# Weight splits issued at a unit's last product, with the loads two units ahead

## The chip, the cores and the metric

The kernel runs on one core of one Trainium2 chip. The time is that of one execution in device microseconds, the median of several executions. The engines named here are TensorE (PE; its weight loads are listed apart as PEld), VectorE (DVE), ScalarE (ACT), GpSimd (POOL) and SyncE (SP), which in this kernel issues the DMAs.

## What is computed

One layer of a bidirectional hybrid encoder in float32, on 2048 tokens of 1024 channels. Cut to what matters:

```
h = rmsnorm(x, g_mix)
z = h @ w_in                      # 1024 -> 5648: qk, v, o, gates of the mLSTM, qkv of NA, q of mem, branch gates
h_m   = mlstm forward + mlstm backward, normalised, times sigmoid(o)
h_na  = neighbourhood attention on the 32 x 64 grid, 8 heads
h_mem = cross attention into 256 memory tokens (k, v from mem @ w_mem_kv)
y = g0 * (h_m @ w_proj_mlstm) + g1 * (h_na @ w_proj_na) + g2 * (h_mem @ w_proj_mem)
x = x + y @ w_out
x + square(relu(rmsnorm(x, g_ffn) @ w_up)) @ w_down
```

## The kernel before

**Products in three parts.** Every large product is made at nearly full float32 precision from three faster ones. Each operand is split into a high part (rounded to float32r) and a low part (the rest), and `mm3` (L226) issues high by high (L231), high by low (L232) and low by high (L233). A weight must therefore be split before it can be used.

**Weight units.** The weights of the first two stages lie in HBM as units of 512 KB (128 partitions by 1024 floats; the four `navm` units have 1056). `fetch` (L155) brings one: it takes a raw buffer (tag `wraw`, 3 of them, L164) and a split buffer (tag `wsp`, 5 of them, L165), issues the load on SP (L171), makes the high part on ACT (L175) and the low part on DVE (L176). The load of a unit has to wait until the split three units earlier has read its raw buffer. The split has to wait until the last product with the unit five earlier has been made, since it takes that unit's place.

**Two kinds of units.** For `naqk`, `navm`, `v` and `o`, a set of four units covers 1024 input channels by 512 (528) output channels, and `tok_group` (L471) runs through all four for each of four groups of 128 tokens. So all four units are in use until the last token group; in it, the first unit has its last product after two of the eight steps over k, the second after four, and so on. For `qk` and the branch gates, one unit covers 128 output channels, and `ch_group` (L481) uses it in 8 steps of three matmuls over 512 tokens and is then done with it.

**Stages.** Stage 1 (`phase_1`) runs four blocks of 512 tokens; `block_a` (L490) takes `naqk`, `qk` (4 units), `navm`, `v`, in blocks 2 and 3 the 24 gate units, and `o`. Between the steps of these products `tick` (L106) slips in small pieces of other work: neighbourhood attention (scores, exponentials L1035, transposes copied out at L1052 and L1054, values L1063), memory attention (exponentials L1179) and the norms of q and k. Stage 2 (`phase_2`) makes the gates of blocks 1 and 0 while the mLSTM runs in the ticks. Stage 3 (the projections and the MLP) fetches its units in its own way.

**Order of the work.** PE runs in program order. The order on ACT, DVE, POOL and SP is fixed before the launch by a planner that goes through a time of its own: among the instructions that could start at that time, it gives an engine the one with the lowest number (`cur_priority`, which counts in program order). `fetch` adds `self.later` = 60 to the number of the two split instructions, so that they rank as if they stood 60 instructions further down. Once fixed, every engine works through its list in order: an instruction that must wait holds up those behind it.

**When units are fetched.** `take` (L218) fetches ahead: when it returns n units, it has fetched until 5 more (`AHEAD`) are there. So the five units behind the set that is about to be used stand in the program ahead of that set's first product, loads and splits together, long before the places are free that their splits go into.

**Evictions around the change.** Each group of products ends in PSUM (two banks for `mm` in stage 1) and is copied out by ACT: L503 (`naqk`), L653 (`qk`, into `cz` for the convolution), L518 and L527 (`navm`), L538 (`v`), L555 (`o`), L598 (gates). PE can begin the group after next only once that copy is made.

Of the kernel before, what the change touches and what calls it, by code (L numbers as in the profile page):

```python
# [12 lines left out]
F32 = mybir.dt.float32  # L13
# [21 lines left out]
ORDER_0 = (2, 3, 0, 1)  # L35
WSP, WRAW, AHEAD = 5, 3, 5
NB = S // TB
SCRATCH = 1024
# [41 lines left out]
class Body:  # L80
    def __init__(self, tc, a):
        self.tc, self.nc, self.a = tc, tc.nc, a
        self.n = 0
        self.later, self.ahead = LATER, AHEAD
# [3 lines left out]
        self.wplan, self.wready = self.plan(), []  # L88

# [65 lines left out]
    def fetch(self):  # L155

        nc = self.nc
        entry = self.wplan.pop(0)
        if len(entry) == 3:
            self.wready.append(self.fetch_sums(*entry[:2]))  # L160
            return
        i, nk = entry
        self.n += 1
        raw = self.p_w.tile([128, 1056], F32, name=f"wr_{self.n}", tag="wraw", bufs=WRAW)  # L164
# [3 lines left out]
        raw = raw[:, :n]  # L168

        w = w[:, :2 * n].rearrange("p (k l c) -> p l k c", k=nk, l=2)  # L170
        nc.sync.dma_start(raw, self.a["w_units"][i] if i < first else self.a["w_navm"][i - first])  # L171
# [3 lines left out]
        nc.scalar.activation(w[:, 0], raw, AF.Copy)  # L175
        nc.vector.tensor_tensor(w[:, 1], raw, w[:, 0].bitcast(F32), ALU.subtract)  # L176
        self.tc.cur_priority -= self.later
        self.wready.append(w)

    def fetch_sums(self, i0, i1):  # L180
# [37 lines left out]
    def take(self, n=4):  # L218

        size = lambda: sum(4 if isinstance(w, dict) else 1 for w in self.wready)  # L220
        while (len(self.wready) < n or size() < n + self.ahead) and self.wplan:
            self.fetch()
        w, self.wready = self.wready[:n], self.wready[n:]
        return w

    def mm3(self, out, lhs, rhs, first, last, more=False):  # L226
# [243 lines left out]

    def tok_group(self, lhsT, w, t, cols=slice(0, 512), every=2):  # L471

        p = self.ps("mm")[:, :cols.stop - cols.start]
        for k in range(8):
            wk = w[k // 2]
            self.mm3(p, self.lhs_tok(lhsT, k, t), (wk[:, 0, k % 2, cols], wk[:, 1, k % 2, cols]), k == 0, k == 7)
            if k % every == every - 1:
                self.tick()
        return p

    def ch_group(self, w, rhs, ks=range(8)):  # L481

        p = self.ps("mm")
        for k in ks:
            self.mm3(p, (w[:, 0, k], w[:, 1, k]), (rhs[:, 0, k], rhs[:, 1, k]), k == ks[0], k == ks[-1])
            if k % 2:
                self.tick()
        return p

    def block_a(self, b):  # L490


        nc, a = self.nc, self.a
        hT = self.hT
        w = self.take(4)
        for i, t in enumerate(ORDER_0 if b == 0 else range(4)):
            if i == 0 or b == 0 and i < 3:
                self.trans_x()
            if b == 0 and i == MEM_R:
                self.mem_rms()  # L500
            p = self.tok_group(hT, w, t)
# [13 lines left out]
        for t in range(4):  # L515
# [8 lines left out]
            p = self.tok_group(hT, w, t, slice(256, 528), 4)  # L524
            z = self.t("zm", [128, 256], 4)
# [7 lines left out]
        for t in range(4):  # L533
            if t == PREP_V and b + 1 < NB and b not in GATES_1:
                self.prep_x()
            p = self.tok_group(hT, w, t)
            s = self.ev()
# [10 lines left out]
        for t in range(4):  # L548
            if t:
                self.trans_x()  # L550
            if t < 3:
                self.prep_x()
            p = self.tok_group(hT, w, t)
            s = self.ev()
# [518 lines left out]
    def mem_setup(self):  # L1073
# [7 lines left out]
        for k in range(0, 8, 2):  # L1081
# [129 lines left out]
    def phase_3(self):  # L1211
# [352 lines left out]
```

## Time and profile before

| | |
|---|---|
| median of 3 runs | 3011.54 us (3009.11 to 3012.48) |
| the profiled execution, own time | 3010.98 us |
| its span, first to last instruction | 3009.2 us |
| mean granted TensorE clock | 0.991 |
| DVE busy over the span | 2070.9 us (69%) |
| ACT busy over the span | 1197.8 us (40%) |
| POOL busy over the span | 240.6 us (8%) |

The busy shares are over the whole span. A row of the windows view gives, for one stretch, each engine's busy time with the number of instructions, the granted TensorE clock (1.00 is full speed), the share of time that the DMA engines worked and the rate. In the timeline view a row is start, duration, engine, line, operation, the tiles written and read, the shapes and a count; the bracket at the end gives the idle time of the engine just before, and what ended it. Stage 1 lasts until about 993 us, and the last gate product of the second stage's units is made at about 1413 us.

### The profile page before, as it was taken

What the parts mean: (1) busy time and instruction counts of PE and PEld (TensorE: products, weight loads), DVE (VectorE), ACT (ScalarE), POOL (GpSimd) and SP (SyncE); (2) the same over time, 40 slices, a digit from 0 to 9 for tenths busy, and PEclk for the clock granted to TensorE, in tenths of its full rate; (3) what the DMA queues carried; (4) which work ended last, traced back from release to release, by engine and by line L of the source; (5) the groups of instructions that cost most, each with busy time, mean ns of one, the idle gap of its engine ahead of it and who ended that gap; (6) DMA issues with size and microseconds to landing.
All of it is one profiled execution on the core that took longest, in us unless ns stands there. A gap on an engine that the chain in (4) does not pass through costs nothing.

```text
span 3009.2 us, 41920 instructions
## 1 busy us (share of the span) xinstructions
PE 2923.3 (97%) x15028; PEld 2382.5 (79%) x15028; DVE 2070.9 (69%) x3557; ACT 1197.8 (40%) x2198; POOL 240.6 (8%) x389
## 2 busy tenths in 40 slices
PE   8989999999989889999999999999999999999999
PEld 6878788878877767778888888888778888888887
DVE  6666676457655675764869888765676888885666
ACT  6454544345543343333234333543322433344331
POOL 3020200011000332330000000000000000000000
PEclk9999999999999999999999999999999999999999
DMA  7776668777789766789634444866774444467554
GB/s 269 229 244 198 217 215 256 244 221 213 229 266 287 231 196 211 251 276 320 199 112 165 153 149 151 282 193 226 252 236 138 137 154 154 154 215 230 191 186 165
DMA packets 341713, 632.97 MB, mean 210 GB/s; under 512 B 29345, under 2 KB 151009, under 8 KB 341505
## 3 DMA queue, kind: packets, MB, share of 16 engines
q1 hardware_dynamic: 341504, 630.30, 65.2%
q8 instruction: 118, 1.93, 0.3%
q14 instruction: 91, 0.74, 0.1%
HBM read 453.63 MB, written 176.55 MB: 209 GB/s over the span
## 4 chain that ended last, share of the span: by engine, by line
PE 58%; DVE 2%; DMA 1%; issue 0%; ACT 0%; SPq 0%; POOL 0%; DVEq 0%; ACTq 0%; POOLq 0%
PE mm L231 19%; PE mm L233 18%; PE mm L232 18%; PE pn L861 1%; PE pn L864 1%; PE mm L1327 0%; DMA wr<-in_w_units_dram 0%; PE mx L870 0%; DVE ev L1483 0%; DVE h L899 0%; DMA hf<-s_hf 0%; DVE acc L1476 0%; DMA X<-s_a 0%; DMA og<-s_o 0%; DVE ws L176 0%
## 5 line engine op out<-in xcount | busy, mean ns | idle before, releaser
L231 PE MATMUL mm<-X,ws 128*128 128x512 f32 x1152 | 448.5, 389 | 0.0
L233 PE MATMUL mm<-X,ws 128*128 128x512 f32 x1152 | 448.2, 389 | 0.0
L232 PE MATMUL mm<-X,ws 128*128 128x512 f32 x1152 | 448.1, 389 | 0.0
L231 PE MATMUL mm<-hT,ws 128*128 128x512 f32 x896 | 378.2, 422 | 12.2 <-ACT cz L653 5.5
L233 PE MATMUL mm<-hT,ws 128*128 128x512 f32 x896 | 355.7, 397 | 0.0
L232 PE MATMUL mm<-hT,ws 128*128 128x512 f32 x896 | 354.8, 396 | 0.6 <-DMA hT<-s_hT 0.6
L232 PE MATMUL mm<-X 128*128 128x512 f32 x896 | 348.8, 389 | 4.4 <-DVE X L1450 4.4
L233 PE MATMUL mm<-X 128*128 128x512 f32 x896 | 348.7, 389 | 0.5 <-DVE X L1450 0.5
L231 PE MATMUL mm<-X 128*128 128x512 f32 x896 | 348.6, 389 | 0.0
L176 DVE TENSOR_TENSOR ws<-wr,ws 128x1024 fp32r<-128x1024 f32 (+1 forms) x212 | 260.8, 1236 | 120.1 <-ACT ws L175 119.0
L1449 ACT ACTIVATE X<-X 128x1024 fp32r<-128x1024 f32 x176 | 187.0, 1062 | 322.9 <-DMA X<-s_t 133.4
L1450 DVE TENSOR_TENSOR X<-X 128x1024 fp32r<-128x1024 f32 x176 | 214.4, 1223 | 133.6 <-ACT X L1449 129.1
L175 ACT ACTIVATE ws<-wr 128x1024 fp32r<-128x1024 f32 (+1 forms) x212 | 223.3, 1059 | 157.4 <-PE mm L233 92.3
L231 PE MATMUL mm<-ws,hT 128*128 128x512 f32 (+2 forms) x704 | 262.2, 372 | 4.3 <-ACT cz L653 2.4
L233 PE MATMUL mm<-ws,hT 128*128 128x512 f32 (+2 forms) x704 | 250.9, 356 | 2.1 <-DVE hT L433 2.1
L232 PEld LDWEIGHTS mm<-X,ws 128*128 128x128 f32 x1152 | 216.3, 188 | 44.9
L233 PEld LDWEIGHTS mm<-X,ws 128*128 128x128 f32 x1152 | 216.2, 188 | 44.9
L231 PEld LDWEIGHTS mm<-X,ws 128*128 128x128 f32 x1152 | 216.2, 188 | 44.7
L232 PE MATMUL mm<-ws,hT 128*128 128x512 f32 (+2 forms) x704 | 250.3, 355 | 0.3 <-DVE ws L176 0.3
L201 ACT ACTIVATE ws<-wr 128x512 fp32r<-128x512 f32 x224 | 135.0, 628 | 220.3 <-PE mm L233 139.7
L231 PEld LDWEIGHTS mm<-hT,ws 128*128 128x128 f32 x896 | 171.2, 191 | 56.9 <-issue 11.1
L233 PEld LDWEIGHTS mm<-hT,ws 128*128 128x128 f32 x896 | 170.4, 190 | 39.5
(266 smaller groups left out, 4865.2 us busy)
## 6 DMA issues: line engine op xcount, KB each, us to landing
wr<-in_w_units_dram SPq DMA_DIRECT2D x308, 512.0 KB
s_s<-u SPq DMA_DIRECT2D x32, 1024.0 KB
X<-s_s SPq DMA_DIRECT2D x64, 512.0 KB
X<-s_t SPq DMA_DIRECT2D x64, 512.0 KB
s_g<-ev SPq DMA_DIRECT2D x96, 256.0 KB
ev<-s_g SPq DMA_DIRECT2D x96, 256.0 KB
s_a<-u SPq DMA_DIRECT2D x96, 256.0 KB
X<-s_a SPq DMA_DIRECT2D x48, 512.0 KB
```

What stands on the lines that cost most here:

```text
L175: nc.scalar.activation(w[:, 0], raw, AF.Copy)
L176: nc.vector.tensor_tensor(w[:, 1], raw, w[:, 0].bitcast(F32), ALU.subtract)
L201: nc.scalar.activation(hi, src, AF.Copy)
L231: mm(out, lhs[0], rhs[0], start=first, stop=False)
L232: mm(out, lhs[0], rhs[1], start=False, stop=False)
L233: mm(out, lhs[1], rhs[0], start=False, stop=last)
L861: nc.tensor.matmul(pn[h % 2][:, j], pt[:, h], v1[:, h], start=True, stop=first)
L864: nc.tensor.matmul(pn[h % 2][:, j], qw[hp, j], C[hp, j], start=False, stop=True)
L1449: nc.scalar.activation(hi, src, AF.Copy)
L1450: nc.vector.tensor_tensor(lo, src, hi.bitcast(F32), ALU.subtract)
```

## The change

Loading and splitting become two steps. `load` takes a raw buffer and issues the DMA; `fetch` first calls `load` until up to `self.pre` units beyond the one in hand are loaded, and then splits that one. In the first two stages `self.pre` is 2. There `take` fetches only what it returns and lacks, and a new `done` fetches one unit at each place where a unit has had its last product: after every second step of the last token group of a set of four (then with `later` = 0), and at the end of every `ch_group` (with `later` = 60). The instructions, buffers and their numbers stay the same. For the third stage the old way is set again (`pre` = 0, `ahead` = 5). During the memory setup at the start, `take` keeps one unit ahead (`ahead` = 1) in place of five.

```diff
+PRE = 2
-        entry = self.wplan.pop(0)
-        if len(entry) == 3:
+        while len(self.wloaded) <= self.pre and self.wplan and (not self.wloaded or len(self.wplan[0]) == 2):
+            self.load()
+        entry, raw = self.wloaded.pop(0)
+        if raw is None:
             self.wready.append(self.fetch_sums(*entry[:2]))
             return
...
-        nc.sync.dma_start(raw, self.a["w_units"][i] if i < first else self.a["w_navm"][i - first])
...
+    def load(self):
+        entry, raw = self.wplan.pop(0), None
+        if len(entry) == 2:
+            i = entry[0]
+            self.n += 1
+            first = self.a["w_units"].shape[0]
+            raw = self.p_w.tile([128, 1056], F32, name=f"wr_{self.n}", tag="wraw", bufs=WRAW)[:, :1024 if i < first else 1056]
+            self.nc.sync.dma_start(raw, self.a["w_units"][i] if i < first else self.a["w_navm"][i - first])
+        self.wloaded.append((entry, raw))
...
     def take(self, n=4):
+        if self.pre:
+            while len(self.wready) < n:
+                self.fetch()
+            w, self.wready = self.wready[:n], self.wready[n:]
+            return w
...
+    def done(self, urgent=False):
+
+        if self.pre and (self.wplan or self.wloaded):
+            self.later = 0 if urgent else LATER
+            self.fetch()
...
     def tok_group(self, lhsT, w, t, cols=slice(0, 512), every=2, last=False):
...
             if k % every == every - 1:
                 self.tick()
+            if last and k % 2:
+                self.done(True)
...
     def ch_group(self, w, rhs, ks=range(8)):
...
             if k % 2:
                 self.tick()
+        self.done()
         return p
...
     def mem_setup(self):
...
-        self.later = later
+        self.ahead = WSP - 4
         w = self.take(4)
...
+        self.later, self.pre = later, PRE
...
             self.tick()
+            if k % 2:
+                self.done(True)
...
     def phase_3(self):
...
+        self.pre, self.later, self.ahead = 0, LATER, AHEAD
         self.late_gates(lambda: True)
```

`tok_group` is called with `last` set for the last token group of `naqk`, of `v`, of `o` and of the second half of `navm`.

More of the change, by code (lines that the diff above doesn't have):

```diff
@@ L83, in __init__ @@
         self.n = 0
-        self.later, self.ahead = LATER, AHEAD
+        self.later, self.ahead, self.pre = LATER, AHEAD, 0
         self.streams, self.qkq, self.memq, self.aux_end = [], [], [], False
@@ L87, in __init__ @@
         self.jobs = []
-        self.wplan, self.wready = self.plan(), []
+        self.wplan, self.wloaded, self.wready = self.plan(), [], []
     def t(self, tag, shape, bufs, dt=F32):
@@ L163, in fetch @@
         self.n += 1
-        raw = self.p_w.tile([128, 1056], F32, name=f"wr_{self.n}", tag="wraw", bufs=WRAW)
         w = self.p_ws.tile([128, 2112], F32R, name=f"ws_{self.n}", tag="wsp", bufs=WSP)
@@ L167, in fetch @@
         n = 1024 if i < first else 1056
-        raw = raw[:, :n]
         w = w[:, :2 * n].rearrange("p (k l c) -> p l k c", k=nk, l=2)
-        nc.sync.dma_start(raw, self.a["w_units"][i] if i < first else self.a["w_navm"][i - first])
         raw = raw.rearrange("p (k c) -> p k c", k=nk)
@@ L218, in take @@
     def take(self, n=4):
+        if self.pre:
[3 more added lines that the diff above has]
+            return w
         size = lambda: sum(4 if isinstance(w, dict) else 1 for w in self.wready)
-        while (len(self.wready) < n or size() < n + self.ahead) and self.wplan:
+        while (len(self.wready) < n or size() < n + self.ahead) and (self.wplan or self.wloaded):
             self.fetch()
@@ L469, in lhs_tok, with tok_group @@
         return hT[:, 0, k, sl], hT[:, 1, k, sl]
-    def tok_group(self, lhsT, w, t, cols=slice(0, 512), every=2):
+    def tok_group(self, lhsT, w, t, cols=slice(0, 512), every=2, last=False):
         p = self.ps("mm")[:, :cols.stop - cols.start]
@@ L500, in block_a @@
                 self.mem_rms()
-            p = self.tok_group(hT, w, t)
+            p = self.tok_group(hT, w, t, last=i == 3)
             z = self.t("zna", [128, 512], 3)
@@ L523, in block_a @@
                     self.store(self.scr["vna"][half, 8 * b + 2 * t + r], s[p0:p0 + 40])
-            p = self.tok_group(hT, w, t, slice(256, 528), 4)
+            p = self.tok_group(hT, w, t, slice(256, 528), 4, t == 3)
             z = self.t("zm", [128, 256], 4)
@@ L535, in block_a @@
                 self.prep_x()
-            p = self.tok_group(hT, w, t)
+            p = self.tok_group(hT, w, t, last=t == 3)
             s = self.ev()
@@ L552, in block_a @@
                 self.prep_x()
-            p = self.tok_group(hT, w, t)
+            p = self.tok_group(hT, w, t, last=t == 3)
             s = self.ev()
```

## The prediction

> **What bounds the kernel now.** I read the page first, then the windows view by stage, then who PE waited for, and only then single places in the timeline.
>
> ```profile
> span 3009.2 us, 41920 instructions
> PE 2923.3 (97%) x15028; PEld 2382.5 (79%) x15028; DVE 2070.9 (69%) x3557; ACT 1197.8 (40%) x2198; POOL 240.6 (8%) x389
> ```
> ```profile
> 0.00:993.00 993.00, 938.23 (x5802) 767.63 (x5802) 618.33 (x1390) 487.76 (x1016) 110.84 (x217) 0.98 0.77 239
> 993.00:1413.00 420.00, 400.03 (x2183) 304.85 (x2184) 266.03 (x526) 158.33 (x417) 129.72 (x172) 0.98 0.75 241
> 1413.00:3009.00 1596.00, 1585.05 (x7045) 1309.98 (x7043) 1186.55 (x1641) 551.74 (x766) 0.00 (x0) 1.00 0.56 185
> ```
>
> PE bounds it. The part that the change touches, up to 1413 us, has 993 - 938.23 + 420 - 400.03 = 74.7 us of idle PE, and a clock of 0.98 where stage 3 has 1.00. Rows are the stretch, then PE, PEld, DVE, ACT and POOL, then clock, DMA share, GB/s. The whole fund is this: 74.7 us, and about 2% of 1413 us (28 us at most) through the clock. What ended those idle times, up to 1500 us:
>
> ```profile
> PE mx L1063 <- DVE npt L1054: 19.4, 13, 4.6
> PE mm L231 <- ACT cz L653: 7.9, 4, 2.5
> ...
> PE mx L231 <- ACT ws L175: 6.9, 1, 6.9
> PE mx L1030 <- DMA nab<-in_rpb_dram: 5.9, 2, 5.6
> ...
> PE mx L232 <- DVE ws L176: 1.0, 2, 0.6
> ...
> PE mm L232 <- DVE ws L176: 0.3, 1, 0.3
> ```
>
> PE hardly ever waits for a split: apart from the start (6.9 us, 1.0 us) it is 0.3 us. It waits for copies on DVE and ACT, and the splits matter as what stands ahead of these copies in their lists. The group view says how much they hold ACT and DVE (last part: idle before them, and what ended it):
>
> ```profile
> L176 DVE TENSOR_TENSOR ws<-wr,ws 128x1024 fp32r<-128x1024 f32 x167 | 205.5, 1237 | 103.2 <-ACT ws L175 102.2
> L175 ACT ACTIVATE ws<-wr 128x1024 fp32r<-128x1024 f32 x167 | 175.3, 1056 | 95.0 <-DMA wr<-in_w_units_dram 54.6 <-PE mm L233 39.8
> ```
>
> A split costs ACT 1.06 us and DVE 1.24 us, and before 1413 us ACT stood 54.6 us at the head of its list for a load and 39.8 us for PE with a split.
>
> **The change, part by part.** No instruction is added or taken away; three are moved per unit. The number of a split falls back by about one channel group: before, unit u+5 is fetched ahead of the products of u, now behind them. So a copy of the same group, which has its number right behind the group, now goes ahead of the split. The load goes the other way: u+7 is loaded at the end of u, so u+5 at the end of u-2, one unit earlier than at the start of u. On SP it passes the stores and bias loads of a unit. On POOL nothing is passed.
>
> *Split behind the eviction (`qk`, blocks 1 and 2).*
>
> ```profile
> 212.02 1.08 ACT L175 ACTIVATE ws<-wr 128x1056 fp32r<-128x1056 f32 x1
> ...
> 214.44 0.60 ACT L653 ACTIVATE cz<-mm 128x512 f32<-128x512 f32 x1
> ```
> ```profile
> 215.09 0.50 PE L231 MATMUL mm<-hT,ws 128*128 128x512 f32 x1 [2.49 <-ACT cz L653]
> ```
> ```profile
> 365.63 1.08 ACT L175 ACTIVATE ws<-wr 128x1056 fp32r<-128x1056 f32 x1
> ...
> 368.15 0.60 ACT L653 ACTIVATE cz<-mm 128x512 f32<-128x512 f32 x1
> ```
> ```profile
> 368.81 0.50 PE L231 MATMUL mm<-hT,ws 128*128 128x512 f32 x1 [1.62 <-ACT cz L653]
> ```
>
> Here the split waits for the same products as the copy and goes first. Moved behind, it gives back 1.08 us at each place: 2.49 becomes 1.41, 1.62 becomes 0.54. The split itself is for `navm`, two groups later, so nobody waits for it.
>
> What a gap costs beyond itself shows in the granted clock behind it (four stretches of the windows view; the clock is the third number from the end):
>
> ```profile
> 216.25:219.65 3.40, 3.40 (x14) 2.80 (x13) 3.40 (x11) 2.08 (x4) 0.14 (x1) 0.50 0.72 259
> 369.00:372.40 3.40, 3.40 (x20) 2.81 (x19) 3.40 (x10) 1.93 (x6) 0.13 (x1) 1.00 0.55 159
> 875.02:878.43 3.41, 3.41 (x11) 2.48 (x9) 2.60 (x6) 1.03 (x3) 0.00 (x0) 0.50 0.54 153
> 1324.00:1327.40 3.40, 3.40 (x24) 2.65 (x22) 3.40 (x10) 1.72 (x9) 2.47 (x3) 1.00 0.91 267
> ```
>
> After the gap of 2.49 us PE ran 3.40 us at half speed; after 1.62 us it did not. Half of 3.40 is 1.70 us lost. With 1.41 us left this goes: 1.08 + 1.70 + 1.08 = 3.9 us.
>
> [...]
>
> *Split behind the attention copies (372 us).*
>
> ```profile
> 373.98 1.25 DVE L176 TENSOR_TENSOR ws<-wr,ws 128x1056 fp32r<-128x1056 f32 x1
> ...
> 376.89 0.68 DVE L1054 COPY npt<-tr 120x512 f32<-120x512 f32 x1
> ```
> ```profile
> 377.62 1.08 PE L1063 MATMUL mx<-npt,nav 120*32 120x128 f32 x16 [4.56 <-DVE npt L1054]
> ```
>
> DVE does the split ahead of the copy on which PE waits 4.56 us. Behind it: 1.25 us less. The gap stays long, so I count no clock.
>
> *Load one unit earlier (gates).*
>
> ```profile
> 865.47 0.43 SPq L171 DMA_DIRECT2D wr<-in_w_units_dram  x1
> ```
> ```profile
> 871.13 1.06 ACT L175 ACTIVATE ws<-wr 128x1024 fp32r<-128x1024 f32 x1 [3.29 <-DMA wr<-in_w_units_dram]
> ...
> 872.57 0.65 ACT L1035 ACTIVATE nsb<-nsb,sm 128x440 f32<-128x440 f32 x1
> ```
> ```profile
> 874.16 1.14 PE L1063 MATMUL mx<-npt,nav 120*32 120x128 f32 x26 [1.87 <-DVE npt L1054]
> ```
> ```profile
> 912.69 1.06 ACT L175 ACTIVATE ws<-wr 128x1024 fp32r<-128x1024 f32 x1 [1.56 <-DMA wr<-in_w_units_dram]
> ```
> ```profile
> 915.59 0.65 PE L1063 MATMUL mx<-npt,nav 120*32 120x128 f32 x16 [1.54 <-DVE npt L1054]
> ```
> ```profile
> 1321.89 1.06 ACT L175 ACTIVATE ws<-wr 128x1024 fp32r<-128x1024 f32 x1 [6.26 <-DMA wr<-in_w_units_dram]
> ```
> ```profile
> 1323.49 0.66 PE L903 MATMUL tr<-ident,h 128*128 128x128 f32 x4 [1.78 <-ACT de L810]
> ```
>
> The load issued at 865.47 us reached ACT at 871.13, 5.7 us later; meanwhile ACT held up the exponential that the copy and then PE needed. A unit is 24 matmuls. The stretch from 369.00 us, at full clock, holds 20 in 3.40 us, 0.17 us each, short ones among them; so a unit lasts at least 24 x 0.17 = 4.1 us, more than the 3.29 us waited. The wait goes, with the gap and the half-speed window at 875.02: 1.87 + 1.70 = 3.6 us. The other two places, 1.54 and 1.78 us, lie between nothing (an attention copy still waits for its own chain) and all of it, 3.3 us; having no nearer row I take half, 1.7 us.
>
> *Splits at the change from one set to the next.* These had the best possible place, at the head of the list. Now what is ready and has a lower number goes ahead.
>
> ```profile
> 106.83 2.95 ACT L175 ACTIVATE ws<-wr 128x1024 fp32r<-128x1024 f32 x3
> 109.68 0.48 ACT L1179 ACTIVATE me<-mx,sm 128x256 f32<-128x256 f32 x1
> ...
> 110.48 0.22 ACT L1179 ACTIVATION_READ_ACCUMULATOR me<-mx,sm 128x1 f32 x1
> ```
> ```profile
> 109.25 0.50 PE L232 MATMUL mm<-ws,hT 128*128 128x512 f32 x1 [0.32 <-DVE ws L176]
> ```
>
> From `navm` to `v` in block 0 there is no slack: PE waits 0.32 us for the first of three splits made back to back. Two exponentials stand just behind them, 110.48 + 0.22 - 109.68 = 1.02 us. If these come first, PE waits 1.0 us more. There are four such changes, one per block. Lower bound nothing, upper bound two pairs at all four, 4 x 2.04 = 8.2 us. I take one pair at the one place without slack, 1.0 us.
>
> *SP.* The loads now reach SP as soon as a raw buffer is free by the planner's time, and SP stands until it is free in fact. This happens already:
>
> ```profile
> SPq L171 <- DVE ws L176: 113.5, 58, 7.3
> ```
>
> One such wait is 113.5 / 58 = 2.0 us, and the stores and bias loads (L1014) stand behind it; PE already waits 5.9 us for such a bias. Most of it is covered by the double-buffered evictions; without this cover, all of a wait reaches PE. I take one, 2.0 us; the bounds are nothing and three, 6 us.
>
> *The rest costs nothing:* `take` and the memory setup issue the same instructions; raw buffers limit the first loads as before. Stage 3 is set back to the old way.
>
> **The sum:** gains 3.9 + 1.25 + 3.6 + 1.7 = 10.4 us; costs 1.0 + 2.0 = 3.0 us; net -7.4 us. Against the profiled execution's own 3010.98 us that gives 3003.6; it lies 0.56 us below the median of the runs, so 3004.1, said as 3004 us.
>
> **The rivals.**
>
> *A: nothing moves.* The engines' lists come from readiness in the planner's time, and a number decides only between instructions that are ready together. With ACT at 40% there is seldom a choice. For it: the 39.8 us that ACT waits for PE show that splits start as soon as their place is free. Against: 212.02 and 365.63, where a choice existed. Small gains and losses cancel: 3011 us, give or take 6.
>
> *B: the splits come too late; slower.* At the change of sets, two exponential pairs get ahead in all four blocks: 8.2 us, with one half-speed window (the gap then passes 1.87 us) 1.7 us, and none of the gains: 3011.5 + 9.9 = 3021 us. It decides once more than the slack stands ahead of the split, and in block 0 that slack is nothing. For it: 109.25, and DVE with 205.5 us of splits in 1413. Against: the sets are split with `later` = 0.
>
> *C: SP stands.* The early loads hold up bias loads and gate stores: three waits, 6 us, half the gains (5.2 us) and the 1.0 us above: 3011.5 + 1.8 = 3013 us.
>
> *D: no clock comes back.* The half-speed windows have another cause than these gaps, so that shortening 2.49 and 1.87 us leaves them: 3004.1 + 3.4 = 3007.5 us. Against it: both windows at 0.50 begin within 1.2 us of the end of such a gap. [...]
>
> **How the numbers follow.** About 0.2%, 6 us, is what a measurement can tell from no change. The forecast has 0.45 (0.40 below 3005.5, 0.05 within), A 0.25 (0.06, 0.15 and 0.04 faster, within, slower), B 0.17 (slower), C 0.08 (half within, half slower), D 0.05 (within). Faster 0.46, within 0.29, slower 0.25. Low end: all gains with the halved ones whole (12.1), a second window at 377 us (1.7) and no cost, 2997.7, and as much again as the two `cz` gaps that I left out (7.9 - 2.49 - 1.62 = 3.8 us) with a window: 2992. High end: B, 3021. Outside lie some 0.07 below and 0.12 above. The forecast's own range is 2997 to 3007.
>
> **What would show it.** Right: ACT's wait for loads in L175 falls well below 54.6 us; `cz` stands ahead of the split in `qk`; fewer windows at 0.50; PE's waits for L653 and L1054 fall below 27.3 us together. Wrong: new PE waits for L175 or L176 at the first group of `v` or `naqk` (B), for `nab` or L598 (C), or a wait list as before (A).

## The result, and the profile after

| | before | after |
|---|---|---|
| median | 3010.99 us (4 runs, 3009.11 to 3012.48) | 3031.65 us (4 runs, 3030.57 to 3037.03) |
| ratio, 95% interval | | 1.0071 (1.0058 to 1.0084) |
| the profiled execution, own time | 3010.98 us | 3037.03 us |
| its span | 3009.2 us | 3035.3 us |

The change costs 20.7 us by the medians. The forecast was 3004, its range 2992 to 3021. One of the ten executions of g1_gates, an experiment described below, took 7413.52 us; its ratio leaves that execution out, its median does not. The profiled execution of after is the longest of its four, 5.4 us above their median, so losses read from its trace add up to somewhat more than 20.7.

In after's lines L252, L253 and L254 are the three matmuls of `mm3` (L231 to L233 before), L187 is the load, L1078 the copy `npt` on DVE, L1062 the scaled scores `nsb` (L1038 before), L677 `cz`, L622 the gates' eviction. First the windows by stage, of after; the columns are those explained above.

```profile
0.00:993.00 993.00, 935.90 (x5793) 765.04 (x5794) 617.64 (x1388) 484.33 (x1013) 109.24 (x217) 0.98 0.77 237
993.00:1413.00 420.00, 386.82 (x2088) 293.73 (x2087) 272.78 (x526) 156.23 (x413) 132.63 (x172) 0.95 0.72 224
1413.00:3009.00 1596.00, 1591.49 (x7063) 1315.41 (x7062) 1178.24 (x1626) 557.34 (x773) 0.00 (x0) 1.00 0.57 188
```

PE's idle time in the same stretches of time is 57.1 us in place of 54.8, and 33.2 us in place of 20.0, where the clock fell from 0.98 to 0.95. Stage 3 comes later and is otherwise the same. Which engine ended PE's waits up to 1500 us, of after (total, times, longest):

```profile
PE mx L1087 <- DVE npt L1078: 23.3, 14, 4.2
...
PE mm L252 <- DMA hT<-s_hT: 8.8, 3, 7.8
...
PE mm L252 <- ACT cz L677: 5.0, 2, 3.5
PE mx L795 <- DVE C L900: 4.8, 2, 2.8
PE mx L894 <- DVE hm L930: 4.6, 4, 2.6
...
PE mx L850 <- DVE C L900: 4.2, 3, 1.5
PE mm L253 <- DVE ws L176: 3.2, 4, 1.6
```

Three kinds are new or grown: the wait for a DMA of `hT` (8.8 us), those of the mLSTM for `C` and `hm` (4.8 + 4.6 + 4.2 us; 2.7 us before, shown with g6_rank2 below), and those for splits L176 in the main products (3.2 us, 0.3 before). The waits for `cz` and `npt`, which the change was to shorten, are 28.3 us together against 27.3.

What the change does to ACT came out as foreseen. The groups view of 0 to 1413 us, after and then before; behind the last bar is the idle time just before these instructions and what ended it:

```profile
L175 ACT ACTIVATE ws<-wr 128x1024 fp32r<-128x1024 f32 (+1 forms) x180 | 189.6, 1059 | 18.6 <-PE mm L254 8.5 <-DMA wr<-in_w_units_dram 8.2 <-DMA wr<-in_w_navm_dram 1.5
```
```profile
L175 ACT ACTIVATE ws<-wr 128x1024 fp32r<-128x1024 f32 (+1 forms) x183 | 192.6, 1058 | 98.2 <-DMA wr<-in_w_units_dram 54.6 <-PE mm L233 41.6 <-DMA wr<-in_w_navm_dram 1.4
```

ACT's idle time ahead of splits fell from 98.2 to 18.6 us, that for loads from 54.6 to 8.2. That idle time was not what bound the kernel.

**Where the time goes.** Both traces have the same 15028 matmul records in the same order. The start of the n-th of them in one profile, less its start in before's, is the lag of that profile at this point of the work. Worked out so, in us (the points are before's times; the other kernels are described below):

```
point           100   400   450   600   650   700   950  1000  1100  1200  1350  1400
after           6.3   3.4   7.9  12.0  15.9  11.8   5.3   9.9   9.5  12.2  24.4  23.7
e7_memold       1.4  -2.1  -1.5  -2.3   6.5   1.9  -5.2  -0.2  -1.3  -1.6   7.3   6.7
k1_close        0.2  -1.9  -1.3  -1.6   5.0   1.9  -4.5  -8.9  -3.1  -3.1  -0.8  -1.4
g1_gates        1.7  -0.4  -0.4  -1.2   0.2  -2.0  -7.1  -5.9  -6.1  -5.2  -3.8  -3.6
g4_behind      -1.7   1.2   1.5   0.4   0.4   0.3  -1.1  -1.8  -1.5  -1.5   0.6   1.5
g6_rank2       -0.9   1.3   1.4   0.7   1.8   1.0   0.2  -0.2  -0.1   2.4   5.7   8.3
p1_later70     -1.8   3.2   4.7   3.6   3.6   5.9   0.0  -0.1   2.0   2.9   5.8   5.9
p3_later65      0.8  -0.9   3.4   2.3   2.3   0.9  -4.1  -4.3  -4.8  -3.9  -2.7  -3.2
```

Read the row of after: a loss at the start, two between 400 and 600 us, one at 650; then, between 650 and 950 us, 10.6 us come back (most of it where the gates run); then 4.6 us at 1000 us and 12.2 between 1200 and 1350. A lag is that of one execution: from 674 us on, the operations, by their tiles, stand in the same order on ACT, DVE, POOL and SP in after and e7_memold, and yet from 700 to 1400 us the one loses 11.9 us and the other 4.8. So a few us between two rows are no price of a part. Four places, with their lines.

*The start.* ACT, then PE, of after, and ACT of before (timeline view):

```profile
20.27 1.05 ACT L359 ACTIVATE xq<-xstage 128x1024 bf16<-128x1024 f32 x1
...
24.51 1.04 ACT L175 ACTIVATE ws<-wr 128x1024 fp32r<-128x1024 f32 x1
```
```profile
25.60 0.50 PE L252 MATMUL mm<-ws,hT 128*128 128x512 f32 x1 [0.84 <-ACT ws L175]
26.86 0.50 PE L253 MATMUL mm<-ws,hT 128*128 128x512 f32 x1 [0.76 <-DVE ws L176]
```
```profile
19.80 1.05 ACT L175 ACTIVATE ws<-wr 128x1024 fp32r<-128x1024 f32 x1
```

Since `take` now keeps one unit ahead in the memory setup in place of five, three units of the first `naqk` are fetched in the product loop, behind the calls of `prep_x` in the program. So their splits rank behind the norm preparation of the first tokens (L359, L362), which is ready and takes ACT from 20.27 to 24.51. The first products wait for these splits. By 100 us the lag is 6.3 us, one gap of 3.46 us at `cz` with two half-speed windows behind it included (before has 2.36 us there and one window).

*From `o` to `naqk` (block 3).* PE of after:

```profile
662.23 0.50 PE L252 MATMUL mm<-ws,hT 128*128 128x512 f32 x1 [0.37 <-ACT ws L175]
664.36 0.50 PE L253 MATMUL mm<-ws,hT 128*128 128x512 f32 x1 [1.63 <-DVE ws L176]
```

The last split of the set comes too late, 2.0 us. But before had two waits for `nsb` just there, 2.00 us at 653.48 and 2.55 us at 659.68 us, which after does not have: the lag falls again by 700 us.

*The reload of `hT`.* SP's queue and PE of after, then SP and PE of before:

```profile
993.53 3.05 SPq L187 DMA_DIRECT2D wr<-in_w_units_dram  x3
...
997.15 5.89 SPq L589 DMA_DIRECT2D hT<-s_hT  x8
```
```profile
1003.00 0.77 PE L252 MATMUL mm<-hT,ws 128*128 128x512 f32 x1 [7.78 <-DMA hT<-s_hT]
```
```profile
988.16 0.34 SPq L171 DMA_DIRECT2D wr<-in_w_units_dram  x1
988.60 0.45 SPq L565 DMA_DIRECT2D hT<-s_hT  x1
...
990.99 3.51 SPq L565 DMA_DIRECT2D hT<-s_hT  x7
```
```profile
993.17 0.47 PE L231 MATMUL mm<-hT,ws 128*128 128x512 f32 x1 [3.32 <-issue]
994.21 0.58 PE L232 MATMUL mm<-hT,ws 128*128 128x512 f32 x1 [0.56 <-DMA hT<-s_hT]
```

At the end of stage 1 the input of the next gates is brought back in eight pieces, and PE waits for it. In after three loads of weights stand ahead of them on SP, each waiting for the split that frees its raw buffer (3.3 us for the three), and the first of the eight pieces leaves 3.6 us after the first load does. Before there was one load; the first piece left 0.4 us after it and the other seven 2.8 us after it, behind a store. PE waits 7.78 us in place of 3.88 (3.32 + 0.56; what ended the 3.32 us the profile doesn't tell).

*The mLSTM in stage 2.* DVE and PE of after, then DVE of before at the same point of the work:

```profile
1263.36 0.68 DVE L930 TENSOR_TENSOR hm<-tr,hm 128x512 fp32r<-128x512 f32 x1
1264.53 0.69 DVE L916 TENSOR_TENSOR h<-h,hf 128x512 f32<-128x512 f32 x1 [0.48 <-DMA hf<-s_hf]
...
1268.00 1.47 DVE L923 SCALAR_TENSOR_TENSOR h<-h,rs,og 128x128 f32<-128x128 f32 x1 [1.11 <-POOL rs L345]
...
1271.36 0.59 DVE L900 SCALAR_TENSOR_TENSOR C<-C,wb,mx 128x129 f32<-128x129 f32 x2
```
```profile
1272.10 0.38 PE L795 MATMUL mx<-ident,r_m 4*128 4x4 f32 x4 [1.96 <-DVE C L900]
```
```profile
1247.03 0.68 DVE L892 TENSOR_TENSOR h<-h,hf 128x512 f32<-128x512 f32 x1
...
1248.77 0.68 DVE L906 TENSOR_TENSOR hm<-tr,hm 128x512 fp32r<-128x512 f32 x1
```

The next chunk of the mLSTM waits for the state update `C`. On DVE, `C` stands behind `h` (L923), which waits for POOL's `rs`; `rs` is made from ACT's squares of the sum `h` (L916). Before, DVE made that sum ahead of `hm` and of the split, in after behind `hm`: 17.5 us later in its trace than in before's, where PE is 14.7 us later. So the chain ends later for PE, which waits 1.96 us here where it had no wait before. By the three rows of the wait list above such waits are 13.6 us, against 2.7 before.

### The profile page after: what moved, and what is told of

Same layout as the page of the kernel before. It is cut to its first block, busy times and chain, and to the rows that moved or that the text cites. A ratio compares the mean times of both kernels' runs of the same rounds, so it can differ in the third digit from the quotient of the medians.

```text
span 3035.3 us, 41892 instructions
## 1 busy us (share of the span) xinstructions
PE 2934.2 (97%) x15028; PEld 2390.4 (79%) x15028; DVE 2080.5 (69%) x3557; ACT 1197.9 (39%) x2198; POOL 241.9 (8%) x389
## 4 chain that ended last, share of the span: by engine, by line
PE 54%; DVE 1%; DMA 1%; issue 0%; ACT 0%; POOL 0%; SPq 0%; DVEq 0%; ACTq 0%; POOLq 0%
PE mm L252 18%; PE mm L254 18%; PE mm L253 18%; PE mm L1355 0%; DMA hf<-s_hf 0%; DMA wr<-in_w_units_dram 0%; DVE ev L1511 0%; DVE h L923 0%; DMA og<-s_o 0%; DVE acc L1504 0%; PE pn L885 0%; POOL rs L345 0%; DMA X<-s_a 0%; ACT hf L919 0%; DMA v<-s_v 0%
## 5 line engine op out<-in xcount | busy, mean ns | idle before, releaser
L252 PE MATMUL mm<-X,ws 128*128 128x512 f32 x1152 | 448.5, 389 | 0.0
L254 PE MATMUL mm<-X,ws 128*128 128x512 f32 x1152 | 448.2, 389 | 0.0
L253 PE MATMUL mm<-X,ws 128*128 128x512 f32 x1152 | 448.1, 389 | 0.0
L252 PE MATMUL mm<-hT,ws 128*128 128x512 f32 x896 | 381.0, 425 | 12.9 <-DMA hT<-s_hT 8.8
L254 PE MATMUL mm<-hT,ws 128*128 128x512 f32 x896 | 357.3, 399 | 0.0
L253 PE MATMUL mm<-hT,ws 128*128 128x512 f32 x896 | 357.0, 398 | 0.0
L253 PE MATMUL mm<-X 128*128 128x512 f32 x896 | 350.1, 391 | 4.0 <-DVE X L1478 4.0
L254 PE MATMUL mm<-X 128*128 128x512 f32 x896 | 349.8, 390 | 0.5 <-DVE X L1478 0.5
L252 PE MATMUL mm<-X 128*128 128x512 f32 x896 | 349.7, 390 | 0.0
L176 DVE TENSOR_TENSOR ws<-wr,ws 128x1024 fp32r<-128x1024 f32 (+1 forms) x212 | 260.4, 1234 | 113.2 <-ACT ws L175 107.9
L252 PE MATMUL mm<-ws,hT 128*128 128x512 f32 (+2 forms) x704 | 262.0, 372 | 5.5 <-ACT cz L677 3.5
L254 PE MATMUL mm<-ws,hT 128*128 128x512 f32 (+2 forms) x704 | 251.1, 357 | 2.8 <-DVE hT L454 2.8
L253 PE MATMUL mm<-ws,hT 128*128 128x512 f32 (+2 forms) x704 | 250.2, 355 | 3.2 <-DVE ws L176 3.2
L254 PEld LDWEIGHTS mm<-X,ws 128*128 128x128 f32 x1152 | 216.2, 188 | 45.0
L253 PEld LDWEIGHTS mm<-X,ws 128*128 128x128 f32 x1152 | 216.2, 188 | 44.9
L252 PEld LDWEIGHTS mm<-X,ws 128*128 128x128 f32 x1152 | 216.2, 188 | 44.7
L252 PEld LDWEIGHTS mm<-hT,ws 128*128 128x128 f32 x896 | 172.2, 192 | 58.5 <-issue 16.0
L254 PEld LDWEIGHTS mm<-hT,ws 128*128 128x128 f32 x896 | 171.9, 192 | 40.0
```

What stands on the lines that cost most here:

```text
L252: mm(out, lhs[0], rhs[0], start=first, stop=False)
L253: mm(out, lhs[0], rhs[1], start=False, stop=False)
L254: mm(out, lhs[1], rhs[0], start=False, stop=last)
```

## The experiments

Ratios are to runs of the kernel before on the same chip; beside each is its 95% interval. 0.001 is 3.0 us.

**Which half, which step.** In e1_stage1 only stage 1 has the new way, in e2_stage2 only stage 2:

```diff
 def phase_2(self):                     # e1_stage1, from after
+        self.pre, self.later, self.ahead = 0, LATER, AHEAD
 def mem_setup(self):                   # e2_stage2, from after: as before,
 def phase_2(self):                     # and then
+        self.pre = PRE
```

> The new way in stage 1 only; the second stage fetches as before. In the two traces PE's products are 5.4 us later than before at 975 us, 23.7 us later at 1413 us. If the cost lies where the lag grows, this kernel is 5 to 9 us slower than before (3016 to 3020 us), and the wait for the reloaded hT at the first gate of the second stage (7.8 us after the change, 3.3 before) belongs to the second stage. If the cost is one that stage 1 hands on (loads and stores queued at its end), it is 15 us or more slower.

Measured: 3021.12 us, 1.0031 (1.0019 to 1.0042).

> The old way in stage 1, the new way in the second stage only. By the lag, 11 to 18 us slower than before (3022 to 3029 us), with the new PE waits for C (VectorE) and sk (ScalarE) there. If the loss of the second stage is handed on from stage 1, it is within 4 us of before.

Measured: 3018.41 us, 1.0026 (1.0014 to 1.0037). Each stage loses, and the two, 0.0057, make up most of the 0.0071. In e2's profile the lag goes from -2.8 us at 1100 to +8.3 us at 1400. Stage 2, which the prediction had not looked at for losses, has over a third of the whole, though its 8 us are less than the 11 to 18 us expected from the lag.

The change has two steps, the earlier load and the later split. e3_loads has the first (splits fetched by `take` as before and the memory setup as before; of its edit only `done` is shown, which now only loads), e4_pre1 the second (`PRE` = 1, which puts each load where it was):

```diff
 def done(self, urgent=False):          # e3_loads
-            self.later = 0 if urgent else LATER
-            self.fetch()
+            while len(self.wloaded) < self.pre and self.wplan and len(self.wplan[0]) == 2:
+                self.load()
-PRE = 2                                # e4_pre1
+PRE = 1
```

> Loads where the change puts them (two units ahead), splits where they were before. If the early loads on SP are the cost (rival C), 12 to 20 us slower than before, with the waits for hT and the bias of the changed kernel. If the late splits are the cost (rival B), within 4 us of before or faster, since ScalarE's 54.6 us of waits for loads go.

Measured: 3022.61 us, 1.0031 (1.0016 to 1.0046).

> Splits where the change puts them, loads one unit ahead, which is their place of before in the program. If the late splits are the cost, 12 to 25 us slower than before; if the early loads are, within 4 us of before, with ScalarE's waits for loads as large as before (54.6 us or more).

Measured: 3020.76 us, 1.0034 (1.0023 to 1.0046). Either step alone costs 9 to 10 us. So it isn't the loads on SP only (rival C), nor the late splits only (rival B).

**The places seen in the trace.** e5_urgent lifts the rank of the splits at the changes of sets, e6_hT issues the last block's four fetches behind the reload of `hT`, and e8_three does both and splits as before in stage 2:

```diff
-            self.later = 0 if urgent else LATER
+            self.later = -400 if urgent else LATER                          # e5, e8
-            p = self.tok_group(hT, w, t, last=t == 3)
+            p = self.tok_group(hT, w, t, last=t == 3 and b < NB - 1)       # e6, e8
...
                             nc.sync.dma_start(hT[:, l, k:k + 2, ts].bitcast(F32), src[:, l, k:k + 2, ts])
+                    for _ in range(4):
+                        self.done(True)
```

> The changed kernel, but the splits of sets rank 400 instructions earlier, so that they stand at the head of the lists again as they did before. If the lost place is the cost (rival B), the four places where PE waited for a split or behind one (25 to 31 us, 115 to 118, 660 to 665 us) go, and the kernel is 5 to 9 us faster than the changed one (3022 to 3027 us). If the early loads or merely another order are the cost, it stays within 4 us of 3032.

Measured: 3025.09 us, 1.0055 (1.0037 to 1.0073). PE's waits for splits in the main products fall from 3.2 to 1.1 us; the time gains 0.0016, 4.8 us, but the intervals overlap.

> The changed kernel, but in the last block the four fetches at the end of o stand in the program behind the reload of hT for the second stage. If the three loads of weight units that stood ahead of these transfers on SP are the cost there (rival C), PE's wait at the first gate of the second stage falls from 7.8 us to 3 to 4 us and the half-speed windows from three to one or two: 5 to 7 us faster than the changed kernel (3025 to 3027 us). If the reload is late for another reason, the wait stays.

Measured: 3027.42 us, 1.0059 (1.0040 to 1.0078). The place itself is mended; SP's queue and PE of e6_hT:

```profile
995.66 1.70 SPq L589 DMA_DIRECT2D hT<-s_hT  x3
997.45 1.37 SPq L187 DMA_DIRECT2D wr<-in_w_units_dram  x3
```
```profile
996.30 0.47 PE L252 MATMUL mm<-hT,ws 128*128 128x512 f32 x1 [1.78 <-issue]
```

The wait of 7.78 us is 1.78 us. The time gains 0.0012, 3.6 us, which the intervals alone can't tell from nothing.

> The changed kernel with three parts taken back: the rank of the set splits (as e5_urgent), the place of the hT reload (as e6_hT), and the second stage fetches as before. If the losses are those three, what stays is the gain of stage 1's gate loads and copies: 3003 to 3010 us. If the loss is spread over many small reorderings, it stays 5 us or more slower than before (3016 us or more).

Measured: 3017.89 us, 1.0027 (1.0016 to 1.0039). Better than after, but 8 us are left: the second case of the expectation. Something was still unnamed.

**Is it order alone?** Three kernels with nothing of the change, only the splits of the first two stages ranked 70, 50 or 65 instructions further down in place of 60:

```diff
-        self.later, self.ahead = LATER, AHEAD
+        self.later, self.ahead = LATER + 10, AHEAD       # p1; - 10 in p2, + 5 in p3
```

> The kernel of before, where only the number added to a split's rank in the first two stages is 70 in place of 60: the same loads and places, a slightly different order. If any other order costs about as much as the parts of the change did (8 to 10 us each), this is 5 to 12 us slower than before and the loss of the change is that of a changed order, not of its places. If the places matter, it is within 4 us of before.

Measured: 3014.38 us, 1.0011 (0.9999 to 1.0024).

> Before with the splits of the first two stages ranked 50 instructions further down in place of 60; loads and places of the calls as before. No part of the change is in it. If the order of before is nothing special, 3008 to 3014 us, as often below 3011 as above. If a change of order alone costs (the rival that what is left of the loss is no step of the change), 3013 to 3018 us, like the 3014.4 of 70 in place of 60.

Measured: 3014.13 us, 1.0015 (1.0000 to 1.0029).

> Before with 65 in place of 60 in the first two stages. The same question as p2_later50 with a smaller step: 3008 to 3014 us if the order of before is nothing special, 3012 to 3018 us if any other order costs some us.

Measured: 3013.09 us, 1.0015 (1.0000 to 1.0030). Each alone is hardly told from no change; the three agree on 3 to 5 us. So a ratio up to about 1.0015 says nothing yet about a cause, and the 8 us of e8_three are more than this.

**The parts of stage 1.** g1_gates has the new way only in the gates of blocks 2 and 3, g2_groups in the gates and `qk`, g3_sets only in the sets of four and the memory setup. In all three stage 2 splits as before, and in g1 and g2 the memory setup is that of before:

```diff
         if b in GATES_1:                                 # g1_gates, g2_groups
+            self.pre = PRE
             for j in range(24):
...
+        self.pre, self.later, self.ahead = 0, LATER, AHEAD
         w = self.take(4)
...
+        self.pre = PRE                                   # g2_groups, around qk
         for c in range(4):
             self.conv(b, c, self.ch_group(self.take(1)[0], hT))
+        self.pre, self.later = 0, LATER
```

> Before with the new way (load two ahead, split at the end of the group) only inside the gate products of blocks 2 and 3; the sets, qk, the memory setup and stage 2 as before. Theory (the places of loss are the changes of sets, the hT reload and the mLSTM; the gates are where the new way gains): the lag of before shrinks by 5 to 8 us between 700 and 950 us as in the whole change, and nothing is lost elsewhere: 3003 to 3008 us. Rival (any change in the order of ACT, DVE and SP costs some us against before's order, wherever it is made, as 70 in place of 60 did): 3012 to 3018 us.

Measured: 3010.12 us, 1.0001 (0.9987 to 1.0015). Between 700 and 950 us its trace gains 5.2 us of lag. But of the placebos, which load no earlier, p1 and p3 gain 5.9 and 5.0 us there and p2 gains nothing (0.1 us), so this can't be put down to the new way, and in the median nothing of it is seen.

> As g1_gates, and the new way also in the four qk groups of each block; the sets keep the old way. Theory (my prediction's first two gains, 3.9 us in qk and 1.25 us at 372 us, are there when the sets are left alone): 3000 to 3005 us, and below g1_gates. Rival (order alone): 3012 to 3018 us.

Measured: 3021.44 us, 1.0041 (1.0029 to 1.0054). Neither theory had this: `qk` the new way with the sets the old way costs 12 us more than the gates alone. Where they are lost is told at the end.

> The new way only for the sets of four in stage 1 (and the memory setup); qk, the gates and stage 2 split as before. If the changes of sets are what costs (rival B of the prediction, and the places at 25, 664 and 1003 us of the changed kernel): 3018 to 3022 us, with those three gaps there. If qk costs what g2_groups lost against g1_gates and the sets only what any other order does: 3011 to 3015 us.

Measured: 3023.58 us, 1.0045 (1.0028 to 1.0062). It lies above both ranges. The three places stand in its trace too: splits late at 26 us (0.85 and 0.76 us) and at 660 us (3.03 and 0.77 us), and 7.59 us of waiting for the reload of `hT` at 1007 us.

**The first gain by itself.** g4_behind is before with the four splits of `qk` ranked so that each stands right behind its `cz` on ACT, loads and places as they were:

```diff
         for c in range(4):
+            self.later = 150
             self.conv(b, c, self.ch_group(self.take(1)[0], hT))
+        self.later = LATER
```

> Before, with the four splits that are fetched in the qk groups of each block ranked 150 further down in place of 60, so that each stands right behind the eviction cz of its group on ACT; loads and everything else as before. My prediction: 1.08 us less at each of two places and one half-speed window gone, 3.9 us, so 3006 to 3008 us. Theory now (PE comes out of the cz wait earlier only to wait for the attention's normalised scores nsb, whose chain over PE, DVE, ACT and DVE sets the pace there): the gaps at cz are gone, gaps at L1049 <- nsb of 1.5 to 2 us stand in their place, and with the late copies behind them the time is 3011 to 3021 us.

Measured: 3012.93 us, 1.0018 (1.0005 to 1.0031). The gain of 3.9 us is not there; the time is longer by about what the placebos cost. The places, of g4_behind (ACT; DVE; PE) and, last, DVE of before (g4's L1040 is before's L1038, its L1037 before's L1035):

```profile
212.37 0.59 ACT L655 ACTIVATE cz<-mm 128x512 f32<-128x512 f32 x1
212.84 1.09 ACT L175 ACTIVATE ws<-wr 128x1056 fp32r<-128x1056 f32 x1
```
```profile
216.54 0.38 DVE L1040 TENSOR_SCALAR nsb<-nsb,sm 128x320 f32<-128x320 f32 x1
```
```profile
217.07 0.52 PE L1051 MATMUL tr<-ident,nsb 128*120 128x128 f32 x3 [1.96 <-DVE nsb L1040]
...
374.00 0.62 PE L1051 MATMUL tr<-ident,nsb 128*120 128x128 f32 x4 [1.79 <-DVE nsb L1040]
```
```profile
214.99 0.37 DVE L1038 TENSOR_SCALAR nsb<-nsb,sm 128x320 f32<-128x320 f32 x1
```

The copy does go first, and PE no longer waits for `cz`. It comes to the transposes of the attention 2 us later, whose scores `nsb` are not scaled yet, and waits 1.96 us there; at the second place 1.79 us. Before, these waits were 2.49 and 1.62 us: 0.36 us less in all, not 2.16. In the stretch where PE stood at `cz`, DVE had finished `nsb`. Nor did `nsb` keep its own place. Before, ACT made its exponential at 213.00 us, ahead of two exponentials of the memory attention; in g4_behind it comes behind them, at 214.71 us, and DVE scales it at 216.54 in place of 214.99 us, while up to this place PE was only 0.36 us later than before. So some 1.2 us of the wait (1.55 - 0.36) come from `nsb` being later itself.

One gain is there. Behind the second place, g4_behind has the split behind the attention copy on DVE (380.41 us, the copy at 379.21), and PE's wait for it is 3.59 us in place of 4.56: 0.97 of the 1.25 us forecast. In after the split still stands ahead of that copy, and PE waits 4.17 us at 380.90 us; DVE of after:

```profile
377.90 1.26 DVE L176 TENSOR_TENSOR ws<-wr,ws 128x1056 fp32r<-128x1056 f32 x1
...
380.15 0.70 DVE L1078 COPY npt<-tr 120x512 f32<-120x512 f32 x1
```

**The rank in stage 2 by itself.** g6_rank2 is before with the splits of stage 2 ranked 150 in place of 60 further down, which is to put each behind the eviction of its group on ACT:

```diff
 def phase_2(self):
+        self.later = 150
...
+        self.later = LATER
         self.late_gates(lambda: True)
```

> Before, with the splits of stage 2 ranked 150 further down in place of 60, so that each stands behind the eviction of its group; loads and stage 1 as before. If the place behind the eviction is what costs in stage 2: 3016 to 3020 us, with new waits of PE for C and hm between 1250 and 1350 us. If it is order alone: 3011 to 3015 us; if it is the loads two ahead on SP: 3009 to 3013 us.

Measured: 3016.80 us, 1.0023 (1.0010 to 1.0035), at the edge of the first case. The lag grows from -0.1 us at 1100 to 8.3 us at 1400. PE's waits from 1100 to 1413 us, of g6_rank2 and of before:

```profile
PE mx L827 <- DVE C L877: 4.2, 3, 1.5
PE mx L772 <- DVE C L877: 2.8, 2, 1.7
PE mx L871 <- DVE hm L907: 2.6, 3, 1.4
```
```profile
PE mx L870 <- DVE hm L906: 1.4, 3, 0.9
PE tr L903 <- DVE C L876: 0.7, 1, 0.7
...
PE mx L826 <- DVE C L876: 0.6, 2, 0.3
```

9.6 us of waits for `C` and `hm` in place of 2.7: the same waits as in after, from the rank alone. DVE makes `hm` ahead of the sum `h` here too (at 1252.02 and 1252.62 us).

**The memory setup, and the closing sum.** e7_memold is the whole change with the memory setup as before; k1_close is that, and with e6's place for the four fetches and stage 2 as before:

```diff
 def mem_setup(self):                   # e7_memold, k1_close, from after
-        self.ahead = WSP - 4
+        self.later = later
         w = self.take(4)
...
-        self.later, self.pre = later, PRE
...
-            if k % 2:
-                self.done(True)
+        self.pre = PRE
```

> The whole change, with the memory setup fetched as before (five units ahead, the new way from the first naqk on). If the late splits of naqk's units at 25 us cost what the trace shows there: 2.5 to 4 us less than the whole change, 3026 to 3029 us. If the loss of the start is made up later anyway: 3029 to 3033 us.

Measured: 3018.65 us, 1.0032 (1.0020 to 1.0044): 0.0039 less than the whole change, 11.7 us, three times what was expected, and more than the 4.9 us (6.3 - 1.4) by which the lags differ at 100 us. Much of the rest is two later gaps of after that e7 hasn't got: from 400 to 600 us after loses 8.6 us by the lag, e7 gains 0.2. PE and DVE of after, and the first place in PE of e7_memold:

```profile
416.88 1.10 PE L1087 MATMUL mx<-npt,nav 120*32 120x128 f32 x26 [2.58 <-DVE npt L1078]
```
```profile
591.76 1.65 PE L1087 MATMUL mx<-npt,nav 120*32 120x128 f32 x25 [3.07 <-DVE npt L1078]
```
```profile
414.99 0.43 DVE L1173 TENSOR_TENSOR zm<-zm,rs 128x256 f32<-128x256 f32 x1 [0.92 <-POOL rs L345]
...
416.14 0.68 DVE L1078 COPY npt<-tr 120x512 f32<-120x512 f32 x1
```
```profile
408.92 1.06 PE L1087 MATMUL mx<-npt,nav 120*32 120x128 f32 x26 [0.17 <-DVE npt L1078]
```

The two kernels differ in the memory setup alone, but the order of their operations on ACT and DVE still differs at places up to 673 us. At 417 us in after, `npt` stands behind `zm`, which waits 0.92 us for POOL; in e7_memold `npt` comes first (408.18 us, `zm` at 409.59). So an early change of order moves attention copies against the products hundreds of us later, and the 11.7 us are no price of the setup itself: g2_groups has both gaps with the old setup.

> The whole change without three of its parts: the memory setup fetches as before, in the last block the four fetches come behind the reload of hT, and stage 2 splits as before. What is left is the new way for qk, the sets and the gates of stage 1. Taken from the changed kernel's 3031.7 us: the memory setup 11.7 us (e7_memold), stage 2 some 8 us (e2_stage2 alone), the reload 3 to 4 us (e6_hT), so 3007 to 3010 us if the parts add and nothing else is lost. If some 4 us are lost to any change of order (the placebos), or to o's units late for naqk in block 3, 3012 to 3016 us. If the parts overlap, so that one undone already brings the others back: 3016 to 3021 us.

Measured: 3010.60 us, 0.9995 (0.9984 to 1.0007). The three parts, undone together, bring back 0.0076, 22.9 us: the whole loss. This doesn't make each of them the owner of a share: g2_groups has none of the three and loses 12 us. What is left, the new way in `qk`, in the sets and in the gates of stage 1, neither gains nor loses. Single figures overlap: 11.7 (memory setup), 12.0 (stage 2, after against e1_stage1; 7.9 where it is added alone) and 3.6 (reload) make 27.3.

## Why the prediction was wrong

**The rest costs nothing** (`take` and the memory setup issue the same instructions): this step failed most, by 11.7 us, the two later gaps included. The same instructions were issued from another place in the program, so with other numbers; the prediction had set down what a number does, and did not apply it here.

**Stage 2** has no term in the sum but half a gain (1.78 us at 1323). That a split behind an eviction can push other work was priced only at the changes of sets. In stage 2 ACT's and DVE's lists carry the mLSTM's chain, and the rank alone gave 9.6 us of waits for `C` and `hm` in place of 2.7; the runs put stage 2 at 7 to 12 us.

**SP**: one wait of 2.0 us taken, three as the bound. Its mechanism (loads that wait for a raw buffer, with urgent transfers behind them) was right; the place was not the bias loads but the reload of `hT`, 3.9 us more of waiting, and three half-speed windows there (998 us) in place of one (994 us). The term was too small, and rival C, which had this mechanism, was priced at 6 us of waits and given 0.08.

**Splits at the changes of sets**: 1.0 us at `navm` to `v`. That place cost 0.5 us more waiting (0.36 + 0.47 us in after, 0.32 before); the late ones were from the memory setup to the first `naqk` and from `o` to block 3's. Rival B had the mechanism. At 664 us most of the loss came back, since PE had waited there for the attention before.

**Split behind the eviction, 3.9 us**: the split moved as said, the gaps for `cz` at 215 and 369 us went, and the gain did not come. The step that failed is that PE would be free once `cz` is there: the scores `nsb` were late next, by 1.96 and 1.79 us in g4_behind (1.53 and 1.81 us in after), in part because the new order puts them later. Rival A's reading (small gains and losses cancel) fits this part.

**Split behind the attention copies, 1.25 us**: in after the split did not move behind the copy, and PE waits 4.17 us in place of 4.56. The price was near: where the split does stand behind, in g4_behind, the wait is 0.97 us shorter.

**Load one unit earlier, 3.6 + 1.7 us**: the mechanism was right, the gain isn't shown. ACT's idle time for loads fell from 54.6 to 8.2 us, and the matmuls that waited 1.87 us at 874 us and 1.54 us at 915 us wait for nothing in after (884 and 921 us), where another gap of 0.94 us stands at 867 us. Between 700 and 950 us after gains 6.4 us of lag. But e4_pre1, which leaves the loads where they were, gains 8.6 us there, two placebos 5 to 6 us and the third 0.1: such a gain comes without the early loads too, and it can be missing.

**The clock**: the windows at 0.50 that the sum counted as won (216, 875 us) went, and others came; below 1413 us half-speed time is 51.2 us before and 78.5 us after. At half speed `mm3`'s matmuls of 128x512 that follow each other without idle time start every 0.43 us in place of 0.23 us (medians, the same in before and after). So a window of 3.41 us costs an estimated 1.6 us (3.41 x 0.20 / 0.43) where the prediction took 1.70, and the 27.3 us more are at most 12.7 us, part of the losses named above. What stood ahead of these windows is told below.

## What to carry to other kernels

Where a planner orders the engines by program position, a call that is moved is a change of rank for everything it issues, in every stage that makes the call: go through each of them, and through each in-order queue, for what now stands behind it, before any gain is counted. A wait that is removed is worth only its distance to the next chain that ends there, and the same change can move that chain too. Measure a placebo, a kernel with the order disturbed and nothing else, before reading a few us as an effect; and close the sum, by undoing all the parts that were named at once.

## What the runs showed of the hardware

**Where the clock records show half speed.** In each of 19 profiles, up to 1413 us, all the stretches at 0.50 start at one phase of a period of 3.413 us, and last one, two or three periods (in after's records 3.413, 6.827 or 10.240 us); the phase differs from run to run. A cell is here one such period. Cells of before:

```profile
79.72:83.13 3.41, 1.16 (x9) 1.16 (x10) 3.14 (x10) 3.06 (x6) 0.00 (x0) 1.00 0.89 323
83.13:86.54 3.41, 3.41 (x11) 2.37 (x11) 3.34 (x5) 0.61 (x2) 0.00 (x0) 0.50 1.08 295
366.44:369.85 3.41, 1.79 (x9) 1.16 (x8) 3.14 (x9) 3.06 (x10) 0.00 (x0) 1.00 0.80 185
369.85:373.26 3.41, 3.21 (x23) 2.29 (x21) 3.41 (x12) 2.29 (x5) 0.13 (x1) 1.00 0.53 211
```

2.25 us of idle PE in one cell (3.41 - 1.16) was followed by half speed in the next; 1.62 us (3.41 - 1.79) was not. Counted over the 19 profiles, from 10 to 1400 us: of 181 cells with over 2.1 us idle all 181 were followed by one at half speed, of 60 with 1.8 to 2.1 us 53, of 200 with 1.2 to 1.8 us 50, and of 7274 with less than 1.2 us 38. Those 38 were all at half speed themselves; of the 7017 at full speed among the 7274, none was followed by one. So, as the author's estimate from these counts, a gap of 2.5 us costs up to 1.6 us more (one window, as priced above) or nothing, by how it is shared between two cells, and at times twice that (behind 2.56 us at 419 us g2_groups has 6.8 us at half speed). Behind the same gap of 2.49 us for `cz` (at 215 us) before has a stretch at half speed, p2_later50 (at 218 us) has none. That the phase differs between runs may be part of why single runs of before lie between 3002 and 3024 us; this was not tested.

**What stays open.** g2_groups loses its 12 us mostly at three late copies `npt` of the attention: its lag grows by 5.0 us between 320 and 360 us (a wait of 3.88 us for `npt` at 346 us), by 6.5 us from 410 to 440 us (2.56 us at 419 us) and by 4.8 us from 580 to 590 us (3.09 us at 595 us). The last two are after's gaps at 417 and 592 us, with the same order on DVE at the first, `npt` behind `zm`; p3_later65 has that order too (2.35 us at 412 us), e7_memold and k1_close have neither gap. Which change of rank in the planner brings this order, and why k1_close, with `qk` the new way as well, escapes it, is not shown: the orders differ in too many places to name one.
